# Hybrid trunk: raw input transposed at once, its norm applied to the products, and 32-tile products in the MLPs

## The chip, the core and the metric

The kernel runs on one core of one Trainium2 chip. The metric is the device time of one execution in microseconds (us), the median over runs. TensorE (PE) multiplies, VectorE (DVE), ScalarE (ACT) and GpSimd (POOL) work element by element, SyncE (SP) issues most DMAs; ACT and POOL issue some as well.

## The reference, cut to what matters

The input x is 256 tokens by 2048 channels, float32. Two layers follow each other, the first with a gated DeltaNet as token mixer, the second with sparse attention; behind each mixer stands an MLP.

```python
def rms_norm(x, g):
    y = xf * lax.rsqrt(jnp.mean(xf * xf, axis=-1, keepdims=True) + EPS)
    return (y * g.astype(jnp.float32)).astype(x.dtype)
...
    for i in range(DEPTH):
        u = rms_norm(h, norm_mix[i])
        if i % N_MIXERS == 0:
            mix = gated_deltanet(u, ...)
        else:
            mix = dsa_attention(u, ...)
        h = h + mix
        h = h + squared_relu_mlp(rms_norm(h, norm_mlp[i]), mlp_w_up[i], mlp_w_down[i])
    return rms_norm(h, norm_final)
```

In gated_deltanet the normed input is multiplied by w_in (12352 columns: q, k and v for a convolution and the delta rule, z for a gate, b and a for beta and decay). The factor rsqrt(mean) is one number per token, so it can be applied to x or to the products of x.

## The kernel before, in words

**Products.** Each weight and each activation is split into a rounded part and a rest ("hi" and "lo": whi, wlo, xhi, xlo), and a product is three matmuls (mm3, L321). by_channel (L359) holds weights stationary and streams 256 tokens: columns of 256, tiles named acc<-xhi,whi and the like. by_token (L377) holds activations stationary and streams weight columns: 512 wide (acc<-whi,h), or 256 wide for z.

**Weights.** Stream (L131) lists every weight block in order of use, 512 KB each. get() (L144) hands out the next one; on the way it issues the DMA of blocks further on (SP, tile raw), casts raw to whi on ACT and subtracts on DVE for wlo, three blocks ahead of use (four buffers each).

**Start.** Scope "first" (L402) loads x in four pieces of 128 x 1024 through SP, the identity, eight rows of gains, and then weights. It sums squares of all four pieces, computes rsqrt, scales x (normalise, L444), and a background generator first (L451) transposes 16 blocks k on PE, splitting each into xhi and xlo with the gain as factor. by_channel of group 0 uses the blocks as they come.

**DeltaNet.** 16 groups g of two heads (L736): by_channel gives q, k, v (192 matmuls), which ACT copies to s; by_token gives z (96 matmuls); group 0 has also the b and a columns (48 matmuls, read by decays, L480). The delta rule itself runs as background generators: delta (L520) per group, solved (L598) per pair of groups. solved inverts a triangular matrix with 32x32 and 64x64 products (aux<-Tc,yv, aux<-Lc,Tct and others), forms the output (the tile Tt), computes a factor f by rsqrt on POOL, multiplies Tt by f and the gate zg on DVE, transposes it on PE (aux<-wide,Tt) and splits it to the tile h.

**What sets the order.** Pace (L28) keeps a modelled clock per engine while the program is written. Background.tick (L122), called after each weight row of a product, emits the next step of a background chain when the model says that its inputs are there. ensure (L345) emits steps regardless, when a product needs their result now. Every engine then runs its instructions in the order in which they were written.

**After the groups.** early_chunks (L396) starts the output projection (512 wide, 6 matmuls per block k) on the 28 first blocks while the last pair is still solved; block 24 is the first that needs pair 6. Then come the MLP (mlp, L829: two halves, each of eight by_channel passes of 192 matmuls and four by_token chunks), the attention layer with its own products, and the second MLP. In the first pass of the first half, transposes of the last chunk (transposed, L787) are still mixed with the matmuls.

Of the kernel before, what the change touches and what calls it, by code (L numbers as in the profile page):

```python
# [14 lines left out]
P = 128  # L15
T = 256
# [114 lines left out]
class Stream:  # L131
# [8 lines left out]
    def add(self, shape, pieces, turn=None):  # L140

        self.items.append((shape, pieces, turn))

    def get(self):  # L144
        pace, i = self.pace, self.used
        self.used += 1
        ahead = min(self.ahead, i + 1)
        while self.split < min(i + ahead + 1, len(self.items)) or self.loaded < min(i + self.loads + 1, len(self.items)):
            while self.loaded < min(self.split + self.loads - self.ahead, len(self.items)):
                (n, w), pieces, _ = self.items[self.loaded]  # L150
                raw = self.raw_pool.tile([P, 1024], F32, name="raw")
                view = raw[:, : n * w].rearrange("p (n w) -> p n w", n=n)
                for at, src in pieces:
                    self.sync.dma_start(out=at(view), in_=src)
                self.raw[self.loaded] = raw
                self.loaded += 1
# [20 lines left out]
def tile_hybrid_trunk(ctx: ExitStack, tc: tile.TileContext, a: dict, out: bass.AP):  # L177
# [115 lines left out]
    def small_tile(n, name, dt=F32):  # L293
        return small.tile([P, n], dt, name=name)
# [104 lines left out]
        return [by_token(2, h_part(tiles), key, outs=o, k0=nk - 4) for o in outs]  # L399


    with tc.tile_pool(name="first", bufs=1) as fp:  # L402
        xin = fp.tile([P, 2, D], F32, name="xin")
        rows = fp.tile([P, P], F32, name="rows")
        cwr = fp.tile([P, 2, P], F32, name="cwr")
        quarters = [(tb, slice(c * 1024, c * 1024 + 1024)) for c in range(2) for tb in range(2)]
        for tb, s in quarters:
            sync.dma_start(out=xin[:, tb, s], in_=a["x"][0, tb * P:tb * P + P, s])
        sync.dma_start(out=ident, in_=a["consts"][:, 0:P])
        dve.memset(rows, 0.0)  # L410
        at = 0
        VEC = {}
        for name, src in (
            ("mix0", a["norm_mix"][0]), ("mlp0", a["norm_mlp"][0]), ("mix1", a["norm_mix"][1]), ("mlp1", a["norm_mlp"][1]),
            ("q", a["dsa_q_norm"][0]), ("kv", a["dsa_kv_norm"][0]), ("kidx", a["dsa_kidx_norm"][0]), ("out", a["dn_out_norm"][0]),
        ):
            n = src.shape[0] // P
            sync.dma_start(out=rows[at:at + n, :], in_=src.rearrange("(n p) -> n p", p=P))
            VEC[name] = at
            at += n  # L420
        pool.dma_start(out=cwr, in_=a["dn_conv_w"][0].rearrange("t (c p) -> (t c) p", p=P).rearrange("(n q) p -> q n p", q=P))
        pool.dma_start(out=upper, in_=a["consts"][:, P:2 * P])
        pool.dma_start(out=fine, in_=a["consts"][:, 2 * P:].rearrange("p (n c) -> p n c", c=B))

        def vec(name, i=0):
            return vecs[:, VEC[name] + i:VEC[name] + i + 1]

        sq4 = small_tile(4, "sq4")
        for n, (tb, s) in enumerate(quarters):
            junk = fp.tile([P, 1024], F32, name="junk", bufs=2)  # L430
            if n % 2 == 0:
                act.activation(junk, xin[:, tb, s], AF.Square, accum_out=sq4[:, n:n + 1])
            else:
                dve.scalar_tensor_tensor(junk, xin[:, tb, s], 1.0, xin[:, tb, s], op0=OP.mult, op1=OP.mult, accum_out=sq4[:, n:n + 1])
        rs = small_tile(2, "rs")
        sq = small_tile(2, "sq")
        dve.tensor_tensor(sq, sq4[:, 0:2], sq4[:, 2:4], op=OP.add)
        dve.tensor_scalar(sq, sq, 1.0 / D, EPS, op0=OP.mult, op1=OP.add)
        rsqrt(rs, sq, 2)
        tp = aux()  # L440
        pe.transpose(tp[:, 0:P], rows, ident)
        act.copy(vecs, tp[:, 0:72])

        def normalise(c):  # L444
            s = slice(c * 512, c * 512 + 512)
            act.activation(xin[:, 0, s], xin[:, 0, s], AF.Copy, scale=rs[:, 0:1])
            dve.tensor_scalar(xin[:, 1, s], xin[:, 1, s], rs[:, 1:2], None, op0=OP.mult)

        normalise(0)

        def first():  # L451
            for k in range(KD):
                t = aux()
                for tb in range(2):
                    pe.transpose(t[:, tb * P:tb * P + P], xin[:, tb, k * P:k * P + P], ident)
                split(t[:, :T], xT[0][:, k], xT[1][:, k], vec("mix0", k))
                ready.add(("x0", k))
                if k % 4 == 1 and k < 12:
                    normalise(k // 4 + 1)
                yield  # L460
            t = aux()
            for i in range(2):
                pe.transpose(t[:, i * P:i * P + P], cwr[:, i, :], ident)
            act.copy(cw, t[:, 0:T])

        bg.add(first())
        bg.step()
        bg.step()
        first_banks = by_channel(8, x_part, "x0", ahead=3)
        bg.drain()  # L470


    tokc = const.tile([P, 2, P], F32, name="tokc")
    GLM, BETA, GL = 32, 64, 96
    hT = []
    with tc.tile_pool(name="delta", bufs=2, reuse_waits="tile") as dp:
        gl_dram = dramp.tile([DN_H, T], F32, name="gl_dram")
        pairs = {}

        def decays(ps):  # L480
            q = slice(96, 128)
# [5 lines left out]
            act.activation(ba[64:96], ps[64:96, :T], AF.Tanh, scale=0.5)  # L487
# [3 lines left out]
            dve.tensor_scalar(xa, ps[q, :T], par[q, 1:2], None, op0=OP.add)  # L491
# [106 lines left out]
        def solved(p, la, r, rs, zg):  # L598
# [159 lines left out]
        chunks = early_chunks(hT, "o", 32, [[pkp.tile([P, 512], F32, name=f"pk{b}") for b in range(2)]])  # L758
        bg.drain()


    res = ctx.enter_context(tc.tile_pool(name="res", bufs=1, reuse_waits="tile"))
    x_scope = x_pool()
# [34 lines left out]
    def finish(outs, part, k0, scale, final):  # L798
# [6 lines left out]
        for tb in range(2):  # L805
# [20 lines left out]
            dve.scalar_tensor_tensor(x, x, rs, final[:, s], op0=OP.mult, op1=OP.mult)  # L826
            (act if tb else sync).dma_start(out=o, in_=x)

    def mlp(key, gain, next_key, final=None):  # L829
# [276 lines left out]
```

## Time and profile before

| | us |
|---|---|
| median of 3 runs (lowest, highest) | 2602.39 (2600.97, 2603.22) |
| the profiled execution | 2600.29 |
| its span in the trace | 2598.4 |
| PE busy | 2555.5 (98%) |
| DVE busy | 1535.6 (59%) |
| ACT busy | 1273.0 (49%) |
| POOL busy | 300.5 (12%) |

A matmul's end in the trace is modelled and overlaps the next one, so the distance from start to start is read as its cost. Stretches of the span: start and group 0 up to some 60 us, DeltaNet groups to 720 us, output projection to 933 us, first MLP to 1457 us and its last chunks to 1660 us, attention layer to 1884 us, second MLP to the end.

### The profile page before, as it was taken

The page shows a single profiled execution, that of the slowest core. Times are in us where ns is not written, and L with a number is a line of the kernel's source. Part 1 is how long each engine was busy: PE and PEld are TensorE (multiplying, and loading weights), DVE is VectorE, ACT ScalarE, POOL GpSimd, SP SyncE. Part 2 cuts the span into 40 slices and gives each one's busy share as a digit, 9 for nine tenths or more (in the row PEclk, how much of TensorE's full clock was granted, in tenths as well). Part 3 has the DMA queues.
Part 4 walks back from the last instruction along what each step waited for, and adds up shares of the span by engine and source line. Part 5 has one row for each costly group of instructions (what it writes and reads, how often), then busy time and mean ns, then how long its engine had stood idle before and what let it go on. Part 6 is the DMA issues. An engine that isn't in the chain of part 4 may idle for free.

```text
span 2598.4 us, 52409 instructions
## 1 busy us (share of the span) xinstructions
PE 2555.5 (98%) x21795; PEld 2342.0 (90%) x21795; DVE 1535.6 (59%) x2179; ACT 1273.0 (49%) x1890; POOL 300.5 (12%) x512
## 2 busy tenths in 40 slices
PE   7999999999999999999999999999999999999998
PEld 7999999999978799988899988898899988999886
DVE  5867677768764555554455555576555544455544
ACT  5555555555554544443344444566454433444443
POOL 0433344434331000000000000000000000000000
PEclk9999999999999999999999999999999999999999
DMA  6755555555554566666666666644666666666664
GB/s 193 195 148 152 143 146 157 146 154 151 153 167 145 173 192 193 194 192 194 194 186 180 194 187 191 183 131 146 177 189 194 194 194 193 189 187 185 193 194 150
DMA packets 325965, 455.91 MB, mean 175 GB/s; under 512 B 18344, under 2 KB 159904, under 8 KB 325344
## 3 DMA queue, kind: packets, MB, share of 16 engines
q1 hardware_dynamic: 322320, 444.11, 57.5%
q10 hardware_dynamic: 3072, 7.11, 0.9%
q8 instruction: 170, 2.79, 0.4%
q0 software_dynamic: 336, 1.34, 0.1%
q14 instruction: 67, 0.55, 0.1%
HBM read 450.37 MB, written 2.13 MB: 174 GB/s over the span
## 4 chain that ended last, share of the span: by engine, by line
PE 90%; DVE 5%; ACT 2%; issue 2%; DMA 1%; POOL 1%; SPq 0%; ACTq 0%; DVEq 0%; POOLq 0%
PE acc L81 81%; PE aux L81 5%; PE pk L81 3%; DVE wlo L81 2%; DVE Tct L81 1%; DVE y L81 1%; ACT Lc L81 1%; ACT whi L81 1%; DMA raw<-in_dn_w_in 0%; POOL rs_u L81 0%; DMA xin<-in_x 0%; POOL E L81 0%; DVE p L81 0%; DVE h L81 0%; DVE Tt L81 0%
## 5 line engine op out<-in xcount | busy, mean ns | idle before, releaser
L81 DVE TENSOR_TENSOR wlo<-raw,whi 128x1024 fp32r<-128x1024 f32 x838 | 1026.8, 1233 | 868.3 <-ACT whi L81 863.2
L81 ACT CAST whi<-raw 128x1024 fp32r<-128x1024 f32 x838 | 874.4, 1049 | 864.8 <-PE acc L81 815.8
L81 PE MATMUL acc<-xhi,whi 128*128 128x256 f32 x3088 | 870.5, 282 | 0.3 <-ACT whi L81 0.3
L81 PE MATMUL acc<-xhi,wlo 128*128 128x256 f32 x3088 | 860.1, 279 | 1.3 <-DVE wlo L81 1.3
L81 PE MATMUL acc<-xlo,whi 128*128 128x256 f32 x3088 | 860.2, 279 | 0.0
L81 PE MATMUL acc<-whi,h 128*128 128x512 f32 x2688 | 846.4, 392 | 4.0 <-ACT acc L81 2.0
L81 PEld LDWEIGHTS acc<-whi,h 128*128 128x128 f32 x2688 | 504.5, 188 | 111.3 <-ACT acc L81 2.9
L81 PEld LDWEIGHTS acc<-xhi,wlo 128*128 128x128 f32 x3088 | 584.7, 189 | 1.8 <-DVE wlo L81 1.8
L81 PEld LDWEIGHTS acc<-xhi,whi 128*128 128x128 f32 x3088 | 580.8, 188 | 2.8 <-ACT whi L81 0.7
L81 PEld LDWEIGHTS acc<-xlo,whi 128*128 128x128 f32 x3088 | 581.7, 188 | 0.2
L81 PE MATMUL acc<-wlo,h 128*128 128x512 f32 x1344 | 524.3, 390 | 0.0
L81 PEld LDWEIGHTS acc<-wlo,h 128*128 128x128 f32 x1344 | 252.6, 188 | 50.0
L81 PE MATMUL acc<-whi,xhi 128*128 128x256 f32 (+2 forms) x576 | 171.3, 297 | 0.0
L81 PE MATMUL acc<-whi,xlo 128*128 128x256 f32 (+2 forms) x576 | 166.1, 288 | 0.0
L81 PE MATMUL acc<-wlo,xhi 128*128 128x256 f32 (+2 forms) x576 | 165.9, 288 | 0.0
L81 POOL TENSOR_SCALAR E<-R,tokc 128x128 f32<-128x128 f32 x96 | 104.1, 1098 | 143.5 <-ACT y L81 79.2
L81 POOL DMA_DIRECT2D gain<-in_norm_final x1 | 0.6, 649 | 956.6 <-DVE nm L81 956.6
L81 PEld LDWEIGHTS acc<-whi,xhi 128*128 128x128 f32 x576 | 108.1, 188 | 2.6
L81 PEld LDWEIGHTS acc<-whi,xlo 128*128 128x128 f32 x576 | 108.2, 188 | 1.2
L81 PEld LDWEIGHTS acc<-wlo,xhi 128*128 128x128 f32 x576 | 108.1, 188 | 1.3
L81 DVE SCALAR_TENSOR_TENSOR y<-s,cw,y 128x255 f32<-128x255 f32 (+2 forms) x192 | 93.9, 489 | 13.1 <-ACT y L81 8.4
L81 POOL TENSOR_TENSOR h<-h,gain 128x512 f32<-128x512 f32 x6 | 7.6, 1290 | 736.5 <-ACT acc L81 736.5
(253 smaller groups left out, 1940.4 us busy)
## 6 DMA issues: line engine op xcount, KB each, us to landing
raw<-in_mlp_w_up SPq DMA_DIRECT2D x256, 512.0 KB, 4.4
raw<-in_mlp_w_down SPq DMA_DIRECT2D x256, 512.0 KB, 4.2
raw<-in_dn_w_in SPq DMA_DIRECT2D x66, 512.0 KB, 4.4
raw<-in_dn_w_in SPq DMA_DIRECT2D x256, 128.0 KB, 2.7
raw<-in_dn_w_in SPq DMA_DIRECT2D x128, 256.0 KB, 3.3
raw<-in_dn_w_out SPq DMA_DIRECT2D x64, 512.0 KB, 3.7
raw<-in_dsa_w_out SPq DMA_DIRECT2D x32, 512.0 KB, 3.9
raw<-in_dsa_w_uq SPq DMA_DIRECT2D x16, 512.0 KB, 3.7
```

Source lines behind the costliest of these rows:

```text
L81: r = f(*args, **kwargs)
```

## The change

Four edits.

1. x is loaded in four blocks of 512 channels for all tokens, the first through SP, three through ACT, whose queue also takes the first gains and the identity; the other gains go through POOL. Weight loads are issued on SP right behind the first block (fetch).
2. x is transposed raw. The squares and rsqrt run in the background behind the 16 transposes. The factor of a token is applied later: as a row (rs_row, made by a product of ones and a diagonal matrix) when q, k and v are taken from the banks (now on DVE) and in decays, as a scale of the tanh of z (rs_half), and as one more POOL multiplication of f in solved (rs0).
3. b, a and z of group 0 are computed inside the first scope, ahead of the taking of q, k and v. 20 products of ones are put on PE: 12 at the very start, 8 behind the first two transposed blocks.
4. In each MLP half one "visit" is put into the background: four 32x32 products whose result is read by nobody.

```diff
+    def fetch(self):
+        while self.loaded < min(self.split + self.loads - self.ahead, len(self.items)):
...
+                self.sync.dma_start(out=at(view), in_=src)
...
+        warm_up(12)
+        act.dma_start(out=rows[0], in_=a["norm_mix"][0].rearrange("(n p) -> n p", p=P))
+        act.dma_start(out=ident, in_=a["consts"][:, 0:P])
+        for c in range(4):
+            (act if c else sync).dma_start(out=xin[:, :, c * 512:c * 512 + 512],
+                                           in_=a["x"][0].rearrange("(b p) d -> p b d", p=P)[:, :, c * 512:c * 512 + 512])
...
+        ws.fetch()
...
-            if n % 2 == 0:
-                act.activation(junk, xin[:, tb, s], AF.Square, accum_out=sq4[:, n:n + 1])
-            else:
-                dve.scalar_tensor_tensor(junk, xin[:, tb, s], 1.0, xin[:, tb, s], op0=OP.mult, op1=OP.mult, accum_out=sq4[:, n:n + 1])
...
-        def normalise(c):
...
-            act.activation(xin[:, 0, s], xin[:, 0, s], AF.Copy, scale=rs[:, 0:1])
-            dve.tensor_scalar(xin[:, 1, s], xin[:, 1, s], rs[:, 1:2], None, op0=OP.mult)
...
+            for c in range(4):
+                squares(c)
+                yield
...
+            rsqrt(rs0, sq, 2)
+            dg = fp.tile([P, 2, P], F32, name="dg")
+            for tb in range(2):
+                dve.tensor_scalar(dg[:, tb], ident, rs0[:, tb:tb + 1], None, op0=OP.mult)
+            yield
+            t = aux()
+            pe.matmul(t[:, :T], lhsT=ones, rhs=dg.rearrange("p b c -> p (b c)"), start=True, stop=True)
+            act.copy(rs_row, t[:, :T])
...
         bg.step()
         bg.step()
+        warm_up(8)
         first_banks = by_channel(8, x_part, "x0", ahead=3)
+        first_ba = by_channel(2, x_part, "x0", n_ct=1)[0]
+        first_zo = by_token(4, x_part, "x0", n_cols=256)
         bg.drain()
...
+            pool.tensor_tensor(four(f), four(f), rs0.unsqueeze(1).unsqueeze(1).to_broadcast([P, 2, 2, 2]), op=OP.mult)
...
-                act.copy(s[:, 2 * c:2 * c + 2].rearrange("p n t -> p (n t)"), banks[c])
+                dve.tensor_tensor(s[:, 2 * c:2 * c + 2], banks[c].rearrange("p (n t) -> p n t", n=2),
+                                  rs_row.unsqueeze(1).to_broadcast([P, 2, T]), op=OP.mult)
             if g == 0:
-                bg.add(decays(by_channel(2, x_part, "x0", n_ct=1)[0]))
-            zo = by_token(4, x_part, "x0", n_cols=256)
+                bg.add(decays(first_ba))
+            zo = by_token(4, x_part, "x0", n_cols=256) if g else first_zo
...
-                act.activation(zg[:, b], zo[b], AF.Tanh, scale=0.5)
+                act.activation(zg[:, b], zo[b], AF.Tanh, scale=rs_half[:, b:b + 1])
...
+    def visit():
+
+        t = aux()
+        for q in range(4):
+            s = slice(B * q, B * q + B)
+            pe.matmul(t[s, 0:B], lhsT=ident[s, s], rhs=ident[s, s], start=True, stop=True)
+        yield
+
     def mlp(key, gain, next_key, final=None):
...
             for p in range(8):
+                if p == 1 - half:
+                    bg.add(visit())
                 banks = by_channel(8, x_part, key)
```

The start on ACT, before (junk is the sum of squares, xin<-xin the scaling by the norm, whi a weight's cast):

```order
L81 ACT_TABLE_LOAD
L81 ACTIVATE junk,sq_117<-xin 128x1024 x2
L81 COPY vecs<-aux 128x72
L81 ACTIVATE xin<-xin,rs 128x512
L81 ACTIVATE xhi<-aux,vecs 128x256 x2
L81 ACTIVATE xin<-xin,rs 128x512
L81 CAST whi<-raw 128x1024 x2
```

and in the change:

```order
L81 DMA rows_105<-in_norm_mix 16x128
L81 DMA wide<-in_consts 128x128
L81 DMA xin<-in_x 128x2x512 x3
L81 ACT_TABLE_LOAD
L81 COPY vecs<-aux 128x16
L81 ACTIVATE xhi<-aux,vecs 128x256 x2
L81 CAST whi<-raw 128x1024 x2
```

Squares and scaling are gone from ahead of the first weight cast; three loads of x are issued here.

The end of pair 6 on DVE, before (sc to f make the factor of the output, Tt<-Tt,f,zg applies it, h is the split that the projection reads, wlo a weight's rest):

```order
L81 TENSOR_TENSOR wlo<-raw,whi 128x1024 x4
L81 TENSOR_SCALAR sc<-rs_9310 128x2
L81 TENSOR_SCALAR sc<-rs_10162 128x2
L81 SCALAR_TENSOR_TENSOR s_11255<-sc 128x4
L81 TENSOR_TENSOR so<-so,s_11255 128x8
L81 TENSOR_SCALAR so<-so 128x8
L81 TENSOR_SCALAR rs_t<-so 128x8
L81 TENSOR_SCALAR f<-rs_t 128x8
L81 TENSOR_TENSOR wlo<-raw,whi 128x1024 x3
L81 SCALAR_TENSOR_TENSOR Tt<-Tt,f,zg 128x128 x8
L81 TENSOR_TENSOR wlo<-raw,whi 128x1024
L81 SCALAR_TENSOR_TENSOR h<-aux,vecs,h 128x512
```

and in the change:

```order
L81 TENSOR_TENSOR wlo<-raw,whi 128x1024 x4
L81 TENSOR_SCALAR sc<-rs_9550 128x2
L81 TENSOR_SCALAR sc<-rs_10311 128x2
L81 SCALAR_TENSOR_TENSOR s_11362<-sc 128x4
L81 TENSOR_TENSOR so<-so,s_11362 128x8
L81 TENSOR_SCALAR so<-so 128x8
L81 TENSOR_SCALAR rs_t<-so 128x8
L81 TENSOR_SCALAR f<-rs_t 128x8
L81 SCALAR_TENSOR_TENSOR Tt<-Tt,f,zg 128x128 x8
L81 SCALAR_TENSOR_TENSOR h<-aux,vecs,h 128x512
```

The four weight rests that stood among these steps are no longer there. PE in the change, at the same place, from the last output products of pair 6 (aux<-yv,la) to its transposes:

```order
L81 MATMUL aux<-yv,la_10374 128x128 x2
L81 MATMUL aux<-yv,la_10375 128x128
L81 MATMUL acc<-whi,h 128x512
L81 MATMUL acc<-wlo,h 128x512
L81 MATMUL acc<-whi,h 128x512 x2
L81 MATMUL acc<-wlo,h 128x512
L81 MATMUL acc<-whi,h 128x512
L81 MATMUL aux<-wide,Tt 128x128 x4
```

Six matmuls of the projection stand between the two; before, 54 did. The transposes stand ahead of block 24 of the projection in both.

## Rows read from the trace of the kernel before

**Rows 1.** Stretches, acc alone: us, PE busy (count), PEld, DVE, ACT, PEclk (granted clock), DMA, GB/s
```profile
20.04:22.62 2.58, 2.50 (x10) 2.28 (x11) 0.00 (x0) 0.00 (x0) 1.00 0.64 165
1000.00:1050.00 50.00, 50.00 (x444) 50.00 (x443) 3.48 (x6) 2.98 (x5) 1.00 0.59 181
1350.00:1400.00 50.00, 50.00 (x427) 50.00 (x426) 4.13 (x6) 3.21 (x6) 1.00 0.59 181
2350.00:2400.00 50.00, 50.00 (x427) 50.00 (x426) 2.75 (x4) 2.38 (x4) 1.00 0.59 178
```

**Rows 2.** Timeline of PE around 32-tile products: start, us, instruction, count
```profile
137.65 0.28 PE L81 MATMUL acc<-xhi,wlo 128*128 128x256 f32 x1
...
139.06 0.28 PE L81 MATMUL acc<-xhi,wlo 128*128 128x256 f32 x1
139.27 0.75 PE L81 MATMUL aux<-Tc,yv 32*32 32x32 f32 x64
...
140.17 0.28 PE L81 MATMUL acc<-xlo,whi 128*128 128x256 f32 x1
...
141.32 0.28 PE L81 MATMUL acc<-xhi,wlo 128*128 128x256 f32 x1
...
696.89 0.75 PE L81 MATMUL aux<-Lc,Tct 32*32 32x32 f32 x64
```

**Rows 3.** Timelines of DVE, ACT and PE at the start
```profile
6.61 1.22 DVE L81 SCALAR_TENSOR_TENSOR junk<-xin 128x1024 f32<-128x1024 f32 x1 [5.48 <-DMA xin<-in_x]
...
10.87 1.22 DVE L81 SCALAR_TENSOR_TENSOR junk<-xin 128x1024 f32<-128x1024 f32 x1 [3.03 <-DMA xin<-in_x]
...
18.76 2.36 DVE L81 TENSOR_TENSOR wlo<-raw,whi 128x1024 fp32r<-128x1024 f32 x2 [0.64 <-ACT whi L81]
...
17.69 1.99 ACT L81 CAST whi<-raw 128x1024 fp32r<-128x1024 f32 x2
...
20.04 0.58 PE L81 MATMUL acc<-xhi,wlo 128*128 128x256 f32 x1 [0.46 <-DVE wlo L81]
...
22.62 0.56 PE L81 MATMUL acc<-xhi,whi 128*128 128x256 f32 x1
...
24.31 0.38 PE L81 MATMUL aux<-wide,xin 128*128 128x128 f32 x2
...
25.92 0.38 PE L81 MATMUL aux<-wide,xin 128*128 128x128 f32 x2
```

**Rows 4.** DeltaNet, 100 to 720 us: two groups of instructions, PE's waits; timeline at 77 us
```profile
L81 ACT COPY s<-acc 128x512 f32<-128x512 f32 x28 | 15.5, 583 | 7.2 <-PE acc L81 6.5
...
L81 DVE SCALAR_TENSOR_TENSOR la<-E,wj,pk 128x512 f32<-128x512 f32 x29 | 20.2, 737 | 0.0
...
PE aux L81 <- DVE Tc L81: 5.9, 9, 1.6
...
77.04 0.44 PE L81 MATMUL aux<-wide,E 128*128 128x128 f32 x2 [1.49 <-DVE E L81]
```

**Rows 5.** Timelines of PE, ACT, POOL and DVE at the end of pair 6
```profile
747.18 1.50 PE L81 MATMUL aux<-yv,la 128*128 128x128 f32 x12
748.44 0.48 PE L81 MATMUL acc<-whi,h 128*128 128x512 f32 x1
...
761.16 1.03 PE L81 MATMUL aux<-wide,Tt 128*128 128x128 f32 x4 [0.22 <-DVE Tt L81]
...
764.71 0.73 PE L81 MATMUL acc<-whi,h 128*128 128x512 f32 x2 [1.01 <-DVE h L81]
...
748.72 0.59 ACT L81 COPY Tt<-aux 128x512 f32<-128x512 f32 x1 [1.24 <-PE aux L81]
...
754.06 1.13 POOL L81 TENSOR_TENSOR rs_u<-f 128x8 f32<-128x8 f32 x1 [13.84 <-DVE f L81]
...
759.41 1.22 POOL L81 TENSOR_TENSOR f<-f,sc 128x8 f32<-128x8 f32 x1
...
760.66 2.19 DVE L81 SCALAR_TENSOR_TENSOR Tt<-Tt,f,zg 128x128 f32<-128x128 f32 x8
```

More of the change, by code (lines that the diff above doesn't have):

```diff
@@ L142, in add @@
         self.items.append((shape, pieces, turn))
+    def fetch(self):
+        while self.loaded < min(self.split + self.loads - self.ahead, len(self.items)):
+            (n, w), pieces, _ = self.items[self.loaded]
+            raw = self.raw_pool.tile([P, 1024], F32, name="raw")
+            view = raw[:, : n * w].rearrange("p (n w) -> p n w", n=n)
+            for at, src in pieces:
+                self.sync.dma_start(out=at(view), in_=src)
+            self.raw[self.loaded] = raw
+            self.loaded += 1
     def get(self):
@@ L148, in get @@
         while self.split < min(i + ahead + 1, len(self.items)) or self.loaded < min(i + self.loads + 1, len(self.items)):
[L149 to L156, printed above, removed]
+            self.fetch()
             if self.split >= min(i + ahead + 1, len(self.items)):
@@ L399, in early_chunks, with warm_up, vec @@
         return [by_token(2, h_part(tiles), key, outs=o, k0=nk - 4) for o in outs]
+    carry = ExitStack()
+    carried = carry.enter_context(tc.tile_pool(name="carried", bufs=1))
+    tokc = carried.tile([P, 2, P], F32, name="tokc")
+    rs0 = carried.tile([P, 2], F32, name="rs0")
+    rs_half = carried.tile([P, 2], F32, name="rs_half")
+    rs_row = carried.tile([P, T], F32, name="rs_row")
     with tc.tile_pool(name="first", bufs=1) as fp:
         xin = fp.tile([P, 2, D], F32, name="xin")
-        rows = fp.tile([P, P], F32, name="rows")
+        rows = [fp.tile([n, P], F32, name=f"rows{n}") for n in (16, 56)]
         cwr = fp.tile([P, 2, P], F32, name="cwr")
[L406 to L410, printed above, removed]
+        def warm_up(n):
+            warm = aux()
+            for _ in range(n):
+                pe.matmul(warm[:, 0:P], lhsT=ones, rhs=ones, start=True, stop=True)
+        warm_up(12)
[4 more added lines that the diff above has]
+                                           in_=a["x"][0].rearrange("(b p) d -> p b d", p=P)[:, :, c * 512:c * 512 + 512])
+        pool.dma_start(out=cwr, in_=a["dn_conv_w"][0].rearrange("t (c p) -> (t c) p", p=P).rearrange("(n q) p -> q n p", q=P))
+        pool.dma_start(out=upper, in_=a["consts"][:, P:2 * P])
+        pool.dma_start(out=fine, in_=a["consts"][:, 2 * P:].rearrange("p (n c) -> p n c", c=B))
+        def vec(name, i=0):
+            return vecs[:, VEC[name] + i:VEC[name] + i + 1]
+        sq8 = small_tile(8, "sq8")
+        ws.fetch()
         at = 0
@@ L417, in tile_hybrid_trunk, with vectors, squares @@
             n = src.shape[0] // P
-            sync.dma_start(out=rows[at:at + n, :], in_=src.rearrange("(n p) -> n p", p=P))
+            if at:
+                pool.dma_start(out=rows[1][at - 16:at - 16 + n, :], in_=src.rearrange("(n p) -> n p", p=P))
             VEC[name] = at
             at += n
[L421 to L430, printed above, removed]
-            if n % 2 == 0:
-                act.activation(junk, xin[:, tb, s], AF.Square, accum_out=sq4[:, n:n + 1])
-            else:
-                dve.scalar_tensor_tensor(junk, xin[:, tb, s], 1.0, xin[:, tb, s], op0=OP.mult, op1=OP.mult, accum_out=sq4[:, n:n + 1])
[L435 to L442, printed above, removed]
-        def normalise(c):
+        def vectors(i, s):
+            tp = aux()
+            n = s.stop - s.start
+            pe.transpose(tp[:, 0:n], rows[i], ident[0:n, 0:n])
+            act.copy(vecs[:, s], tp[:, 0:n])
+        vectors(0, slice(0, 16))
+        def squares(c):
             s = slice(c * 512, c * 512 + 512)
-            act.activation(xin[:, 0, s], xin[:, 0, s], AF.Copy, scale=rs[:, 0:1])
-            dve.tensor_scalar(xin[:, 1, s], xin[:, 1, s], rs[:, 1:2], None, op0=OP.mult)
-        normalise(0)
+            junk = fp.tile([P, 2, 512], F32, name="junk", bufs=2)
+            act.activation(junk[:, 0], xin[:, 0, s], AF.Square, accum_out=sq8[:, c:c + 1])
+            dve.scalar_tensor_tensor(junk[:, 1], xin[:, 1, s], 1.0, xin[:, 1, s], op0=OP.mult, op1=OP.mult,
+                                     accum_out=sq8[:, 4 + c:5 + c])
         def first():
@@ L457, in first @@
                 ready.add(("x0", k))
-                if k % 4 == 1 and k < 12:
-                    normalise(k // 4 + 1)
                 yield
+            for c in range(4):
+                squares(c)
+                yield
+            sq = small_tile(2, "sq")
+            dve.tensor_reduce(sq, sq8.rearrange("p (b c) -> p b c", b=2), axis=AX.X, op=OP.add)
+            dve.tensor_scalar(sq, sq, 1.0 / D, EPS, op0=OP.mult, op1=OP.add)
+            rsqrt(rs0, sq, 2)
[7 more added lines that the diff above has]
+            yield
             t = aux()
@@ L464, in first @@
             act.copy(cw, t[:, 0:T])
+            vectors(1, slice(16, 72))
         bg.add(first())
@@ L468, in tile_hybrid_trunk @@
         bg.step()
+        warm_up(8)
         first_banks = by_channel(8, x_part, "x0", ahead=3)
+        first_ba = by_channel(2, x_part, "x0", n_ct=1)[0]
+        first_zo = by_token(4, x_part, "x0", n_cols=256)
         bg.drain()
-    tokc = const.tile([P, 2, P], F32, name="tokc")
     GLM, BETA, GL = 32, 64, 96
@@ L478, in tile_hybrid_trunk @@
         pairs = {}
+        dve.tensor_scalar(rs_half, rs0, 0.5, None, op0=OP.mult)
         def decays(ps):
@@ L486, in decays @@
             dve.memset(ba, 0.0)
-            act.activation(ba[64:96], ps[64:96, :T], AF.Tanh, scale=0.5)
+            dve.tensor_tensor(ba[64:96], ps[64:96, :T], rs_row[64:96], op=OP.mult)
+            act.activation(ba[64:96], ba[64:96], AF.Tanh, scale=0.5)
             dve.tensor_scalar(ba[64:96], ba[64:96], 0.5, 0.5, op0=OP.mult, op1=OP.add)
@@ L490, in decays @@
             xa, e, z, p = (w[q, i] for i in range(4))
-            dve.tensor_scalar(xa, ps[q, :T], par[q, 1:2], None, op0=OP.add)
+            dve.tensor_tensor(xa, ps[q, :T], rs_row[q], op=OP.mult)
+            dve.tensor_scalar(xa, xa, par[q, 1:2], None, op0=OP.add)
             dve.scalar_tensor_tensor(e, xa, -1.0, xa, op0=OP.mult, op1=OP.max)
@@ L759, in tile_hybrid_trunk @@
         bg.drain()
+    carry.close()
     res = ctx.enter_context(tc.tile_pool(name="res", bufs=1, reuse_waits="tile"))
@@ L827, in finish @@
             (act if tb else sync).dma_start(out=o, in_=x)
+    def visit():
[3 more added lines that the diff above has]
+            pe.matmul(t[s, 0:B], lhsT=ident[s, s], rhs=ident[s, s], start=True, stop=True)
+        yield
     def mlp(key, gain, next_key, final=None):
```

## The prediction, made before the change was run

> **What bounds the kernel now.** I read the table of busy times first: PE is busy for 98% of the span, the next engine (DVE) for 59%. So a change moves the time only through the number of matmuls, the distance between them, or the few places where PE stands still. Then the stretches of acc matmuls, for the distance. In the first half of an MLP 444 matmuls start in 50 us, 112.6 ns each; in the second half 427, 117.1 ns each, in the first MLP and in the second alike [rows 1]. The granted clock is 1.00 in all of them, so the 4.5 ns are not the clock. The reader should see that PE is full in both and still has two paces. Then PE's timeline around 32x32 products in DeltaNet: 12 matmuls take 1.41 us ahead of them (137.65 to 139.06, 117.5 ns each), and the ten distances behind (140.17 to 141.32) are 115 ns with the first, slower ones among them [rows 2]. I went through 28 such places from 139.27 to 696.89 us, these two being the first and the last. Where the same kind of matmul goes on, the short distance follows in 26. Most (22) had it already, but of the five that came at the long distance four left at the short one. Last, the timelines of the start, of DeltaNet's waits and of the end of pair 6 [rows 3, 4, 5].
>
> **The start.** Before, PE flows from 20.04, released by the first weight rest: whi 1.0 us (two in 1.99), then wlo 1.2 us (two in 2.36) [rows 3]. The weights were issued behind x, the norm and the gains. Of x, the second piece of 512 KB was in use at 6.61 and the fourth at 10.87 [rows 3], so 1 MB takes 4.3 us. In the change the weights follow the first megabyte of x on SP while ACT's queue brings the other three blocks beside them. If the queues share evenly, the first weights are there when 2.1 MB have landed, at about 10.9, and 2.2 us of whi and wlo make 13.2: **-6.8**. Ends: weights as soon as the first block, flow at 9.4 (-10.6); weights behind all of x, 15.3 (-4.7). The transposes need one x block, no norm, and are ahead of that. The squares, now beside the matmuls, cost DVE and ACT the same two to four us that they had free.
>
> Between 20.04 and 22.62 ten matmuls and two transposes start in 2.58 us; from 24.31 to 25.92 twelve and two take 1.61 [rows 3]. At the later pace the first set would take 14/12 less, 1.38 us: the slow beginning costs 1.2. The granted clock in that stretch is 1.00 too [rows 1], so only the distances (0.21 us beside 0.11) show it; they look like the lower of the two levels, 1.2 and 2.4 GHz. The change puts 20 products of ones ahead, yet there is still waiting between the last of them and the first wlo. I take half: **-0.6** (0 to -1.2).
>
> **DeltaNet.** The taking of s moves from ACT, 583 ns each, to DVE, where the nearest row of that shape is 737 ns; it is 32 times on either [rows 4], some 24 us on an engine that is 60% busy. PE waited 5.9 us for DVE (nine waits for Tc between 100 and 720 us) [rows 4]. A DVE that has a quarter more to do ahead of these steps makes them later by perhaps a fifth, +1.3; the first taking of a bank in group 1 by 0.15 us for each of four banks, +0.7; the wait of 1.49 for E at 77.04 [rows 4] may vanish, since z, b and a of group 0 now stand ahead, -1.5. Together **+0.5**, ends -3 (the nine waits halve as well) and +6 (they double).
>
> **The end of pair 6.** The last output products of pair 6 begin at 747.18 and the transposes of Tt stand at 761.16, where PE waits only 0.22 us [rows 5]. In between goes a chain: ACT's copy at 748.72, POOL's factor from 754.06 to its last multiplication at 759.41 (1.22 us), DVE's Tt at 760.66. PE covers it with 54 projection matmuls from 748.44 on, 12.50 us without the wait, 0.231 us each. The written order of the change leaves six of them there: the chain is emitted later against PE, the model steps it on time only until block 24 forces it, and block 24 comes first. So 48 matmuls (11.1 us) of cover are gone, and POOL has one more multiplication in the chain (12 steps take 5.35 us from 754.06 to 759.41, so +0.45). What PE no longer does there it does later, hence this is time: +11.55. The wait for h at 764.71, 1.01 us [rows 5], goes, because the weight rest ahead of h is no longer there: **+10.5**. Ends: +8.5, if DVE without its four weight rests is 2 us earlier with Tt; +11.6.
>
> After such a stall PE may come back at the pace of the start, whose price was 1.2 [rows 3]: **+1.2**, ends 0 and +1.4. The Trainium skill, "TensorE: Matmul & The Clock Gate", Part 1, says that the half rate is the default and that an idle PE is put back to it; by that rule the term stands, without it the sum is 1.2 less.
>
> **The visits.** In half 1 the visit stands behind the first 12 matmuls of 1536 and 1524 follow: 2 x 1524 x 4.5 ns = -13.7 [rows 1]. In half 0 the pace is short already, and the visit leaves it so. One visit costs what the 64 products at 139.27 cost beyond their number: from 139.06 to 140.17 pass 1.11 us, less one distance 0.99; 0.75 of it are the 64 (12 ns each, four take 0.05), 0.24 the change over and back [rows 2]. So 0.3 each, 1.2 for four (0.2 to 4.0): **-12.5**. Their aux tile is free and nobody waits for it.
>
> **Sum** against the profiled execution, 2600.3: -6.8 - 0.6 + 0.5 + 10.5 + 1.2 - 12.5 = -7.7, so 2592.6. The median of the runs is 2.1 above that execution: **2594.7 us**. The other edits (rs_half, rs_row in decays) replace an operand, at the same count of instructions, and cost nothing.
>
> **Rivals.**
> (a) Visits only cost. For: in 22 of 26 places the short pace was there before, so the products may have caused nothing. Against: four of five long ones became short. The -13.7 goes: 2608.4. The Trainium skill, "TensorEngine Tiling (Array Packing)", Key Properties, speaks for it: a change of the tiling mode drains PE, and it promises nothing for what follows. The 0.24 us agree with a drain; whether that is all, the trace before cannot say.
> (b) Slower: a visit leaves the long pace wherever it stands. Place: pass 1 of half 0, behind which 1332 matmuls run at the short one in each MLP; it decides if the pace falls with the first matmuls behind the visit. 2 x 1332 x 4.5 ns = 12.0, plus the lost 13.7: 2620.4. For: transposes flip the pace in either direction, and at one place in DeltaNet the long one stayed. Against: 22 of 23 short ones stayed short.
> (c) Mixed: half 1 is mended, half 0 spoiled: 2606.7.
> (d) The stall at pair 6 does not come, or the chain is short: without its 11.7 it is 2583.0. For: the chain may be hidden by something that the written order doesn't show. Against: PE runs in that order, and six matmuls are 1.4 us.
>
> **How the numbers follow.** The forecast with its own range, 2587 to 2602 from the ends above, gets 0.60; (a) 0.15, (b) 0.08, (c) 0.07, (d) 0.10. 0.2% of 2602.4 is 5.2 us, about what a measurement of this kernel can tell from no change: faster is below 2597.2, slower above 2607.6. Faster: (d) 0.10 and most of the forecast, 0.43. Same: the rest of it, 0.17, half of (a) and most of (c), 0.10. Slower: (b), half of (a) and a bit of (c), 0.20. The range 2584 to 2609 leaves out (b) and half of (d), and a little more at either end.
>
> **What the profile after would show.** The first row of steady matmuls near 13.2 us. 444 matmuls per 50 us in both halves of both MLPs; if 427 in half 1, (a) holds; if 427 in half 0, (b) or (c). One wait of PE of 10 to 12 us for Tt near the end of pair 6, and 0.2 us distances behind it. s on DVE near 0.7 us, PE's waits for Tc between 4 and 10 us. Wrong would be the prediction if DVE became what PE waits for in most groups, if the weights landed behind all of x, or if the pace in DeltaNet's own stretches moved, which I did not cost.

## The result, and the profile after

The changed kernel takes 2644.91 us (median of four runs, 2643.84 to 2646.61) against 2602.19 for the one before: 1.0164 times as long, 95% interval 1.0152 to 1.0176. Forecast was 2594.7, a little faster. The page of its profiled execution, span and busy times:

```profile
span 2642.4 us, 52603 instructions
...
PE 2593.6 (98%) x21870; PEld 2369.8 (90%) x21870; DVE 1558.6 (59%) x2215; ACT 1255.9 (48%) x1860; POOL 289.1 (11%) x527
```

PE is as full as before and 38 us longer busy, with 75 matmuls more. Waits are not in the busy time, so the matmuls themselves are slower. The acc stretches of the first MLP after the change, first a stretch of half 0, then one of half 1, with the columns of [rows 1]:

```profile
1000.00:1050.00 50.00, 50.00 (x427) 50.00 (x426) 2.75 (x4) 2.38 (x4) 1.00 0.61 183
1350.00:1400.00 50.00, 50.00 (x427) 50.00 (x426) 2.75 (x4) 2.38 (x4) 1.00 0.62 192
```

Half 0 had 444 in 50 us before [rows 1] and has 427 now; half 1 has 427 still, in spite of its visit. PE's timeline around the visit of half 0 (the four products are recorded as eight):

```profile
983.97 0.28 PE L81 MATMUL acc<-xlo,whi 128*128 128x256 f32 x1
984.09 0.28 PE L81 MATMUL acc<-xhi,wlo 128*128 128x256 f32 x1
984.30 0.26 PE L81 MATMUL pk<-wide 32*32 32x32 f32 x8
984.49 0.39 PE L81 MATMUL acc<-xhi,whi 128*128 128x256 f32 x1
984.71 0.28 PE L81 MATMUL acc<-xlo,whi 128*128 128x256 f32 x1
984.83 0.28 PE L81 MATMUL acc<-xhi,wlo 128*128 128x256 f32 x1
```

The distance is 0.12 us on either side. So half 0 was slow before its visit came; the visit did not make it so, and did not mend it. From 984.09 to 984.49 pass 0.40 us, less one distance 0.28, and the next matmul is 0.1 us late: the visit costs some 0.4 us, where 0.3 was forecast.

The start, timelines of ACT and PE:

```profile
10.84 1.05 ACT L81 CAST whi<-raw 128x1024 fp32r<-128x1024 f32 x1 [1.76 <-DMA raw<-in_dn_w_in]
14.19 1.05 ACT L81 CAST whi<-raw 128x1024 fp32r<-128x1024 f32 x1 [2.31 <-DMA raw<-in_dn_w_in]
...
13.20 0.39 PE L81 MATMUL acc<-xhi,wlo 128*128 128x256 f32 x1 [0.75 <-DVE wlo L81]
...
16.95 0.44 PE L81 MATMUL aux<-wide,xin 128*128 128x128 f32 x2 [2.31 <-DVE xlo L81]
...
18.25 0.41 PE L81 MATMUL acc<-xhi,whi 128*128 128x256 f32 x1
18.46 0.42 PE L81 MATMUL acc<-xlo,whi 128*128 128x256 f32 x1
```

The first weights are there at 10.84 (forecast 10.9) and the flow begins at 13.20 (forecast 13.2; 20.04 before, [rows 3]). But the second weights come only at 14.19; ACT, which waits for them, cannot make the next xhi, PE stands still for 2.31 us, and behind that the distance is 0.21 us. The stretches of that place and of the one behind the stall of pair 6 (us, PE busy, PEld, DVE, ACT, POOL, then the granted clock, DMA share and GB/s):

```profile
17.60:20.60 3.00, 3.00 (x17) 3.00 (x16) 2.22 (x3) 2.58 (x4) 0.00 (x0) 0.50 0.81 228
...
787.87:790.00 2.13, 2.13 (x5) 1.66 (x6) 0.73 (x1) 0.00 (x0) 0.00 (x0) 0.50 0.00 0
```

Here the granted clock is 0.50, the lower of the two levels, each time behind a wait of PE. The first of the two is no fixed part of the change: in a_pad896 (below), which has the same instructions in the same order, PE waits 2.06 us at this place and the clock stays at 1.00 behind it:

```profile
17.60:20.60 3.00, 3.00 (x29) 3.00 (x28) 2.35 (x3) 2.52 (x5) 0.00 (x0) 1.00 0.74 213
```

The end of pair 6 on PE:

```profile
774.65 1.50 PE L81 MATMUL aux<-yv,la 128*128 128x128 f32 x12
775.90 0.48 PE L81 MATMUL acc<-whi,h 128*128 128x512 f32 x1
...
777.14 0.40 PE L81 MATMUL acc<-whi,h 128*128 128x512 f32 x1
785.92 1.17 PE L81 MATMUL aux<-wide,Tt 128*128 128x128 f32 x4 [8.38 <-DVE Tt L81]
787.87 0.80 PE L81 MATMUL acc<-whi,h 128*128 128x512 f32 x1 [0.78 <-ACT h L81]
788.46 0.63 PE L81 MATMUL acc<-wlo,h 128*128 128x512 f32 x1
```

Six matmuls stand in the gap, as the written order had it, and PE waits 8.38 us where it waited 0.22 [rows 5]; behind it the matmuls are 0.4 to 0.6 us apart instead of 0.23. The chain behind it is shorter than before, 10.0 us from 775.90 to 785.92 where it was 12.7. POOL's part, first and last step:

```profile
781.52 0.20 POOL L81 TENSOR_TENSOR rs_u<-f 128x8 f32<-128x8 f32 x1 [13.59 <-DVE f L81]
...
785.19 0.20 POOL L81 TENSOR_TENSOR f<-f,rs 128x8 f32<-128x8 f32 x1
```

All 14 steps take 0.20 us. Before, the first and the last took 1.13 and 1.22 [rows 5], and each of the three long ones ran while DVE worked on a weight rest; here no rest stands in the gap. The rests before, and the third long step:

```profile
753.90 1.23 DVE L81 TENSOR_TENSOR wlo<-raw,whi 128x1024 fp32r<-128x1024 f32 x1
756.62 1.23 DVE L81 TENSOR_TENSOR wlo<-raw,whi 128x1024 fp32r<-128x1024 f32 x1 [1.49 <-ACT whi L81]
759.34 1.22 DVE L81 TENSOR_TENSOR wlo<-raw,whi 128x1024 fp32r<-128x1024 f32 x1 [1.49 <-ACT whi L81]
...
756.70 1.21 POOL L81 TENSOR_SCALAR rs_u<-rs_u 128x8 f32<-128x8 f32 x1
```

This holds for the whole trace of the kernel before: the 80 POOL operations of this form that begin while DVE stands free take 0.20 us, the 23 that begin during a weight rest take 1.05 to 1.27 and end 0.06 us behind the rest.

PE's waits between 100 and 720 us (in total, times, longest):

```profile
PE aux L81 <- DVE Tc L81: 9.7, 6, 1.9
PE aux L81 <- DVE Tt L81: 2.6, 6, 0.4
PE acc L81 <- DVE wlo L81: 1.4, 5, 0.5
```

Tc was 5.9 [rows 4].

What the prediction had not looked at is where the tiles stand in memory. The change takes tokc (1024 bytes per partition) out of the pool "const" at the bottom and leaves 128 bytes more in "small"; so raw, whi, wlo and h all stand 896 bytes lower. xhi and xlo hang from the top and stay. The addresses of the built programs, in bytes per partition:

```
            before   change   remainder by 256: before, change
whi         40480    39584    32   160
wlo         56864    55968    32   160
one h      101920   101024    32   160
xhi        172000   172000   224   224
xlo        188384   188384   224   224
```

So whi stood 64 bytes above xhi by the remainder of 256 before the change, and 192 above it (64 below) after; wlo and xlo stand like them.

### The profile page after: what moved, and what is told of

Same layout as the page of the kernel before. It is cut to its first block, busy times and chain, and to the rows that moved or that the text cites. A ratio compares the mean times of both kernels' runs of the same rounds, so it can differ in the third digit from the quotient of the medians.

```text
span 2642.4 us, 52603 instructions
## 1 busy us (share of the span) xinstructions
PE 2593.6 (98%) x21870; PEld 2369.8 (90%) x21870; DVE 1558.6 (59%) x2215; ACT 1255.9 (48%) x1860; POOL 289.1 (11%) x527
## 4 chain that ended last, share of the span: by engine, by line
PE 84%; issue 5%; DVE 5%; POOL 2%; ACT 2%; DMA 1%; SPq 0%; ACTq 0%; DVEq 0%; POOLq 0%
PE acc L81 77%; PE aux L81 4%; PE pk L81 3%; DVE wlo L81 2%; POOL rs_u L81 1%; DVE y L81 1%; DMA raw<-in_dn_w_in 1%; DVE Tct L81 1%; ACT whi L81 1%; POOL E L81 1%; POOL f L81 1%; DVE s L81 0%; DMA xin<-in_x 0%; ACT s L81 0%; ACT Lc L81 0%
## 5 line engine op out<-in xcount | busy, mean ns | idle before, releaser
L81 POOL TENSOR_SCALAR E<-R,tokc 128x128 f32<-128x128 f32 x96 | 96.4, 1017 | 89.3 <-ACT y L81 84.0
```

What stands on the lines that cost most here:

```text
L81: r = f(*args, **kwargs)
```

## The experiments

### Move the tiles alone

```diff
     ones = const.tile([P, P], F32, name="ones")
+    const.tile([P, 224], F32, name="pad")
```

**a_pad896**: the changed kernel with this line. 

> The changed kernel with one unused tile of 896 bytes per partition ahead of the small pool, so that the weight buffers, the tiles h and all pools behind them stand at the addresses of the kernel before (they had moved down by 896 bytes, while xhi and xlo stayed where they were). The instructions and their order do not change. Theory A (the pace of the 256-column matmuls hangs on where the weights stand against xhi and xlo): half 0 of both MLPs runs at 113 ns again, 2 x 6.5 us less, DeltaNet gets back 3 to 5 us of its own pace, the 512-wide stretches 1 to 3 us: 2622 to 2632 us. If the visits work in this layout, half 1 runs at 113 too, and it is 2609 to 2618. Theory B (the visits, or the other order of the work, made half 0 slow): half 0 stays at 117.8, and the time within 3 us of the changed kernel's 2644.9.

**b_low896**: the kernel before, moved the other way.

```diff
+    const.tile([P, 32], F32, name="pad")
...
+    carry = ExitStack()
+    carried = carry.enter_context(tc.tile_pool(name="carried", bufs=1))
+    tokc = carried.tile([P, 2, P], F32, name="tokc")
...
-    tokc = const.tile([P, 2, P], F32, name="tokc")
```

> The kernel before with its weight buffers and the pools behind them moved down by 896 bytes (tokc is taken from a pool of its own behind them, 128 bytes of padding stand ahead), as the change moved them; instructions and order as before. Theory A: half 0 of both MLPs falls to 117.8 ns, 2 x 6.5 us, DeltaNet's own pace loses 3 to 5, the 512-wide stretches 1 to 3: 2619 to 2625 us. Theory B: nothing changes, 2600 to 2604.

Measured: a_pad896 2608.79 us, ratio to before 1.0024 (1.0014 to 1.0033): 36 us of the change are gone with 896 unused bytes. b_low896 2624.03 us, 1.0079 (1.0064 to 1.0094): 21 us more than the kernel before, whose half 1 had no short pace to lose. Their stretches, a_pad896 first:

```profile
1000.00:1050.00 50.00, 50.00 (x444) 50.00 (x443) 3.44 (x5) 2.98 (x5) 1.00 0.58 182
1350.00:1400.00 50.00, 50.00 (x444) 50.00 (x443) 3.04 (x5) 2.38 (x4) 1.00 0.58 184
```

and b_low896:

```profile
1000.00:1050.00 50.00, 50.00 (x427) 50.00 (x426) 2.75 (x4) 2.38 (x4) 1.00 0.63 192
1350.00:1400.00 50.00, 50.00 (x427) 50.00 (x426) 2.75 (x4) 2.38 (x4) 1.00 0.62 193
```

The shift gives and takes half 0's pace in either kernel, with no instruction moved: of the two theories A holds, B is out. In a_pad896 half 1 is at 444 too: at these addresses its visit works. Comparing when the same matmul starts in the changed kernel and in a_pad896, the 35.2 us between their spans come from DeltaNet and what is ahead of it (5.7), half 0 of the two MLPs (7.2 and 7.3), half 1 (7.0 and 6.9), and 1.1 from the rest.

### The visits alone

```diff
             for p in range(8):
+                if p == 1 - half:
+                    bg.add(visit())
```

**a_novisit** leaves these out of the changed kernel, **b_visits** adds them (and visit itself) to the kernel before, nothing else.

> The changed kernel without the four visits. Theory A: the visits do nothing but cost their 0.3 us each, half 0 stays at 117.8 ns without them: 2643 to 2645 us. Theory B: without the visits half 0 is back at 113 ns in its last seven passes: 2631 to 2633.

> The kernel before with the four visits and nothing else. Theory A says nothing on half 1, where the layout allows both paces: if a visit sets the short one, 13.7 less 1.2 is gained, 2589 to 2591 us; if not, it costs 1.2: 2602 to 2605, and half 0 stays at 113. Theory B: half 0 falls to 117.8 behind the visit: 2613 to 2617.

a_novisit: 2642.44 us (2640.35 to 2642.88), ratio 1.0148 (1.0133 to 1.0164), just under theory A's 2643 and 9 us above theory B's 2633. b_visits: 2590.55 us, ratio 0.9951 (0.9936 to 0.9965). The stretches of b_visits:

```profile
1000.00:1050.00 50.00, 50.00 (x444) 50.00 (x443) 4.13 (x6) 3.58 (x6) 1.00 0.61 190
1350.00:1400.00 50.00, 50.00 (x444) 50.00 (x443) 4.13 (x6) 3.57 (x6) 1.00 0.59 187
```

The visits are worth 12.2 us at the addresses of the kernel before, where 12.5 was forecast, and at those of the change they only cost: 2.5 us by the medians, which the two intervals do not tell from the 1.2 forecast. By its median b_visits is the fastest version of all that compute the reference: both kernels are beaten by adding 32-tile products to the old one.

### Which distance is good

My next idea was that the short pace comes when both operands have the same remainder, since the 512-wide matmuls are at 227 ns where theirs agree. Paddings of other sizes (the same line), at first on the kernel before and on the change:

**b_low64.** 

> The kernel before with its weight buffers and all pools behind them 64 bytes lower, made like the run with 896 bytes (other padding), instructions and order as before. Where the addresses stand: xhi, xlo and the last two tiles h at 32 bytes below a multiple of 512, whi, wlo and the other tiles h at 32 above one in the kernel before, at 160 above one in the change, and here at 32 below one, as xhi. In the kernel before the 512-wide matmuls run at 227 ns where both operands have the same remainder, and at 229 to 232 with the last two tiles h. Theory A1 (the short pace comes whenever both operands of a matmul have the same remainder by 512): all halves of both MLPs at 113 ns without any visit, 13.6 less, DeltaNet 5 to 9 less, the 512-wide stretches 1 to 2: 2577 to 2584 us. Theory A2 (a shift only draws the pace of each stretch anew): at least one half, or DeltaNet's own stretches, slower than that: 2590 to 2625.

**a_pad832.** 

> The changed kernel with 832 bytes of padding, which is 64 less than the run with 896: whi, wlo and h have the remainder of xhi. Theory A1: all at the short pace, so 2608.8 less 1 to 5 in DeltaNet and 1 to 2 in the 512-wide stretches: 2601 to 2607 us. Theory A2: anything from 2608 to 2645.

**a_pad576.** 

> The changed kernel with 576 bytes of padding: whi, wlo and h have the remainder of xhi by 256, but not by 512. If 256 is the period, it reads like the run with 832 bytes, 2601 to 2607 us; if not, half 0 and half 1 of the MLPs are at 117.8 ns, about 2645, or mixed between.

It was wrong, and clearly: b_low64 2641.73 us (1.0151, 1.0136 to 1.0166), a_pad832 2657.93 (1.0212, 1.0197 to 1.0227), a_pad576 2659.5 (one execution). The stretch of half 0 in b_low64:

```profile
1000.00:1050.00 50.00, 50.00 (x419) 50.00 (x419) 2.75 (x4) 2.37 (x4) 1.00 0.61 187
```

419 in 50 us, a third pace of 119.3 ns by this count and 120.0 from start to start, in both halves; in a_pad832 DeltaNet's by_channel runs at 120.0 as well. Equal remainders are among the worst places for these matmuls, and in a_pad832 the visits do nothing. a_pad832 and a_pad576 are 256 bytes apart and alike.

The other distances were tried on a_cover (its order is told below; its padding is 896):

**c_pad704.** 

> The run with the new order of the projection, but 704 bytes of padding in place of 896: whi, wlo and h stand 128 bytes away from xhi by remainder of 256. Seen so far: 0 apart, all 256-column matmuls of by_channel at 120.0 ns; 64 above xhi, either 113.3 or 117.8, and a visit sets 113.3; 192 above xhi (64 below), 117.8 nearly always. Theory P1 (the farther apart, the better): 113.3 everywhere, DeltaNet gets its 5.4 us of slower pace back: 2588 to 2592 us. Theory P2 (64 above is a lucky place): slower than 2596.2, up to 2635 where all are at 120.0 or 117.8.

**c_pad864.** 

> The same with 864 bytes: 32 above xhi by remainder of 256. Theory P1: between 0 and 64 apart, so mostly 117.8 to 120.0: 2615 to 2635 us. Theory P2: no order, anything between 2590 and 2635.

**c_pad640.** 

> The new order of the projection with 640 bytes of padding: 64 above xhi by remainder of 256, as with 896, but 256 bytes lower. If the remainder by 256 (or less) decides: MLP halves at 113.3 ns, 2594 to 2599 us. If the whole distance, or a longer period, decides: halves at 117 to 120, 2615 to 2645.

**c_pad672.** 

> The same with 672 bytes: 96 above xhi by remainder of 256. Known: 64 above gives 113.3 with a visit, 128 above 118.7. If a band around 64 is good, 113.3 and 2594 to 2600; if 64 alone, 117 to 119 and 2625 to 2640.

**c_pad736.** 

> The same with 736 bytes: 160 above xhi by remainder of 256, between 128 (118.7 ns) and 192 (117.8). Expected between them, 2628 to 2640 us; if the pairs 64 apart from each other share something, no reason for 113.3 here.

| whi above xhi by remainder of 256 | runs | matmuls in 50 us from 1000 and from 1350 | time of the runs on a_cover, us |
|---|---|---|---|
| 0 | b_low64, a_pad832, a_pad576 | 419, 419 (b_low64) | |
| 32 | c_pad864 | 425, 425 | 2634.06 |
| 64 | before, b_visits, a_pad896, a_cover, c_pad640 | 444, 427 without a visit; 444, 443 or 444 with | 2596.19 and 2596.12 |
| 96 | c_pad672 | 428, 424 | 2636.39 |
| 128 | c_pad704 | 424, 424 | 2638.88 |
| 160 | c_pad736 | 419, 419 | 2650.11 |
| 192 | the change, a_novisit, b_low896 | 427, 427 | |

c_pad864, c_pad640, c_pad672 and c_pad736 are one execution each. c_pad640 stands 256 bytes lower than a_cover and takes the same time, well within the scatter of a_cover's runs (2594.09 to 2597.56): the remainder by 256 decides, not the distance as such. P1 (the farther the better) falls with c_pad704, which is slower than P2's 2635 too, and the band that c_pad672 looked for is not there: of the seven distances tried, 64 alone lets a visit set 113 ns. c_pad736 was expected between its neighbours, at 2628 to 2640, and is slower than both.

In all these runs whi moved and xhi stayed, so whi's own place would explain the table as well. The matmuls of z speak against it. There the activations are stationary and the weights stream, so the distance of the stationary from the moving operand is 192 where by_channel has 64, and 64 where it has 192. I counted, between 100 and 730 us, behind how many groups of 32-tile products (48 or 64 of them) the short pace follows (a median under 116 ns) where the same kind of matmul goes on:

| run | by_channel, distance | short behind | z, distance | short behind |
|---|---|---|---|---|
| before | 64 | 25 of 26 | 192 | 4 of 16 |
| b_low896 | 192 | 3 of 26 | 64 | 16 of 16 |
| a_pad896 | 64 | 31 of 33 | 192 | 3 of 16 |
| the change | 192 | 7 of 33 | 64 | 12 of 16 |

The two kinds change places with the shift. If whi's own place counted, it would have to be good in one role and bad in the other; the stationary operand's distance from the moving one fits both. No run moved xhi. At 160 and 96 it fits as well: at 160 by_channel has 120 ns (MLPs of c_pad736) and z 120 (c_pad672), at 96 by_channel 117 to 119 (c_pad672) and z 118 (c_pad736). For 224, which no run has for by_channel, z in c_pad864 gives 117 ns. Why 64 is good, and why the pace lasts over hundreds of matmuls once it is set, these runs don't tell.

### The end of pair 6

**a_cover**: a_pad896 with the projection in another order.

```diff
+        head = ([(0, 0, 24), (1, 0, 24), (0, 24, 28), (1, 24, 28), (2, 0, 28)] if nk == 32 else [(c, 0, late) for c in early])
...
+        if nk == 32:
+            outs = [by_token(12, h_part(tiles), key) for _ in range(2)]
+            for o in outs:
+                by_token(2, h_part(tiles), key, outs=o, k0=24)
+            outs.append(by_token(14, h_part(tiles), key, outs=banks[0]))
```

> The changed kernel with 896 bytes of padding and another order of the output projection: the first 24 blocks of chunks 0 and 1, then blocks 24 to 27 of both, then chunk 2, so that 144 matmuls more stand ahead of the first use of pair 6. The step of the prediction on pair 6 (a chain that has lost its cover): the wait of 8.4 us for Tt goes to under 1, and the doubled distances behind it too: 2608.8 less 9 to 12, 2597 to 2600 us. The rival (the wait comes from DVE's or POOL's new work, and moves with it): it comes back at another place, 2606 to 2611.

2596.19 us, ratio 0.9971 (0.9961 to 0.9981), 12.6 less than a_pad896. PE's waits between 717 and 960 us, where Tt led the list with 8.4:

```profile
PE aux L81 <- DVE Tc L81: 2.0, 2, 1.5
PE acc L81 <- ACT acc L81: 1.0, 1, 1.0
```

Tt is not among them any more, and it did not come back elsewhere; 12.6 is a little over the 9 to 12 expected. The lost cover is shown as the cause.

### DVE's new load in DeltaNet

**c_sact**: a_cover with the takings of s back on ACT.

```diff
-                dve.tensor_tensor(s[:, 2 * c:2 * c + 2], banks[c].rearrange("p (n t) -> p n t", n=2),
-                                  rs_row.unsqueeze(1).to_broadcast([P, 2, T]), op=OP.mult)
+                act._engine.copy(s[:, 2 * c:2 * c + 2].rearrange("p n t -> p (n t)"), banks[c])
+                pace.note("dve", "tensor_tensor", (s[:, 2 * c:2 * c + 2],), {})
```

(The second line keeps the modelled clocks as they were, so that the order stays.) 

> The run with the new order of the projection, with the 32 takings of s back on ACT, as plain copies; what is left out is the token's factor on q, k and v. The order of PE's instructions and of POOL's is the same, only DVE loses 32 operations of 0.67 us and ACT gets 32 of 0.58. The prediction's step on DeltaNet (DVE's new load delays what PE waits for): PE's waits in DeltaNet go from 17 back to 11 us as before the change: 2596.2 less 5 to 8, 2588 to 2591. The rival (the waits come from the other order of steps, and from more interruptions): within 2 of 2596.2.

2586.38 us, 9.8 less than a_cover. Its waits from 100 to 720 us:

```profile
PE aux L81 <- DVE Tc L81: 7.3, 8, 1.1
PE aux L81 <- DVE Tt L81: 2.6, 6, 0.4
PE aux L81 <- ACT Lc L81: 1.6, 6, 0.7
```

In a_cover they were 9.5 for Tc and 2.7 for wlo. Matmul by matmul, DeltaNet takes 9.7 us less here than in a_cover. Of these 5.8 are waits of PE (17.35 to 11.53 in all of DeltaNet, added up from the trace). Another 1.4 stand from 163.33 to 166.74 us, where a_cover's granted clock reads 0.50 behind a wait of 1.78 us for Tc; here it reads 1.00 all through DeltaNet. The rest I can't assign. DVE's load is shown as the cause of that cost, at more than the 5 to 8 us expected.

**c_pool**: the same plain copies, and the factor applied behind them on POOL.

```diff
+                act.copy(s[:, 2 * c:2 * c + 2].rearrange("p n t -> p (n t)"), banks[c])
+                pool.tensor_tensor(s[:, 2 * c:2 * c + 2], s[:, 2 * c:2 * c + 2],
+                                   rs_row.unsqueeze(1).to_broadcast([P, 2, T]), op=OP.mult)
```

> The run with the new order of the projection (896 bytes of padding), with q, k and v taken from the banks by ACT as plain copies and multiplied by the token's factor on POOL, in place. It computes everything. DVE is as free as in the run with the plain copies (2586.4), POOL gets 32 operations, of 1.05 us or a little more each by its 128x256 rows, at the head of each group's chain. Theory: the chain has that much time to spare, 2586 to 2590 us. Rival: POOL or the longer chain becomes what PE waits for: 2596 or more.

2611.10 us, ratio 1.0028 (1.0018 to 1.0039): the rival. The new operation on POOL, and PE's wait, from 100 to 720 us:

```profile
L81 POOL TENSOR_TENSOR s<-s,rs_row 128x512 f32<-128x512 f32 x26 | 38.1, 1488 | 46.3 <-ACT s L81 46.3
...
PE aux L81 <- DVE Tc L81: 16.3, 7, 3.2
```

Each takes 1.49 us and lies in the chain, and PE's wait for Tc goes from 9.5 to 16.3. All waits of DeltaNet together are 24.2 us, 6.8 more than in a_cover. The larger part of the 14.9 us is the clock: from waits of 1.5 to 3.2 us on the granted clock of DeltaNet reads 0.50 for 27.3 us in all (3.4 in a_cover), PE is busy in 25.5 of them, and at half pace that is, by estimate, 13 us lost against 2. Two of these stretches, the first behind PE's wait of 3.22 us for Tc at 161.04:

```profile
162.18:165.59 3.41, 3.41 (x76) 3.12 (x75) 2.26 (x3) 2.74 (x4) 1.53 (x2) 0.50 0.54 127
...
551.30:554.71 3.41, 3.41 (x76) 3.12 (x75) 2.87 (x4) 3.41 (x5) 0.45 (x1) 0.50 0.70 191
```

The order was planned anew here, so its share isn't told apart.

## Why the prediction was wrong, and where it was right

**The pace of the MLPs** was the step that failed, in both halves of the term for the visits: "In half 0 the pace is short already, and the visit leaves it so", and half 1's -13.7. Both took the short pace as a state that transposes and 32-tile products set. It is that only at some addresses, and the prediction put their shift at nothing, without a look. The change moved whi by 896 bytes against xhi: half 0 fell to 117.8 ns, which costs 14.5 us in the two MLPs; half 1 stayed at 117.8 in spite of its visits, so 13.9 of the forecast gain did not come; and 5.7 were lost ahead of the MLPs, 3.7 in DeltaNet, whose pace suffers too, and 2.0 in the start, where the low clock stands in the one trace and not in the other. The 36 us are shown by moving nothing but the addresses, and b_low896 shows the loss in the other direction. That DeltaNet's own pace might move the prediction had named as a sign of being wrong. Of the rivals, (b) had the price of a spoilt half 0, but from a wrong mechanism: it laid it on the visit, and in the trace the pace is long ahead of it.

The trace of the kernel before held the sign. The prediction's 26 short ones in 28 places fit by_channel (25 of 26 in the count above); for z, with the operands in the other roles, the short pace follows the same products in 4 of 16 places. So the products alone do not set the pace.

**The visits** at the old addresses came out as reckoned: -12.5 forecast, -12.2 measured in the kernel before. Rival (a), that they only cost, holds at the addresses of the change. The rule of the Trainium skill that was put beside it ("TensorEngine Tiling (Array Packing)", Key Properties: a change of the mode drains PE) fits the 0.28 us ahead of the next matmul; a visit's gain, 113 against 118 ns behind it, lies outside that rule.

**DeltaNet** was the second miss, in size: +0.5 (ends -3 and +6) forecast. DVE's 32 new operations alone are worth 9.8 us. I scaled the waits that were there; the load also made new ones (wlo), and a longer wait can put the clock down behind it (the 1.4 us in a_cover). The rs_row in decays, called a replaced operand, is two DVE operations more, once.

**The start** fell short of its ends: -6.8 and -0.6 forecast, -4.7 at the least; where group 0 ends, a_pad896 is 4.5 us ahead of the kernel before and the changed kernel 2.6. The flow began at 13.20 as worked out, and at full pace, but a wait for the second weights gave part back (2.31 us, and 2.06 in a_pad896), and in the changed kernel's trace the 0.50 clock behind it too. The step took the first weight for the whole supply.

**Pair 6** was right in its mechanism: +10.5 and +1.2 forecast, 12.6 measured by giving the cover back. That the sum fits so well is partly luck, since both parts were off. The wait is 8.4, not 11.6: the chain is 2.7 us shorter, near the lower end of the step, but because POOL's steps are no longer slowed beside weight rests, and not because DVE is earlier. 12.6 less the 8.2 by which the wait grew leaves 4.4. In a_pad896 the granted clock is 0.50 for 10.2 us around this place and PE is busy in 6.2 of them, so some 3 us of it (an estimate) are the clock, where 1.2 was allowed; the rest is what else the new order saved. That the clock falls behind an idle PE, as "TensorE: Matmul & The Clock Gate" (Part 1) of the Trainium skill has it, is seen here behind the 8.4 us; behind the waits of some 2 us it is seen in one trace and not in another.

Without the 36 us of the addresses the change is 14 above the forecast: 2.9 from the start, 9.3 from DeltaNet, 0.9 from pair 6 and 0.3 from the visits, which leaves 0.7, less than the runs of a_pad896 scatter (2606.80 to 2613.89).

## What to carry to other kernels

Before costing a change by its instructions, list the addresses of the tiles that PE reads before and after it: a moved constant can slow thousands of matmuls (here those of 256 columns by 4%, while the 512-wide ones stay at 227 to 229 ns), and padding undoes it. Where one kind of matmul has two paces in a trace, treat the pace as something that the layout allows, and try some paddings of 32 bytes apart before anything else. A chain written by a modelled clock needs its cover counted again whenever work ahead of it moves. And where a change makes waits of PE longer, look at the granted clock behind them, not only at the waits.

## What the runs showed of the hardware

Four things that I had not expected. The distance of 256-column matmuls (weights whi or wlo, moving xhi or xlo) hangs on where the two stand by the remainder of 256 bytes: in the MLP halves 120.0 ns at 0 apart, 113.3 or 117.8 at 64, 117.8 at 192, and at no other distance tried 113.3 for a whole half. At 64 the pace is set by what PE did just before: behind a visit 113.3 ns for the 1524 matmuls that follow, without one 117.8 for all 1536 (half 1 of b_visits and of the kernel before). POOL's 128x8 operations took 0.20 us alone and 1.05 to 1.27 where a weight rest of 1.23 us ran on DVE at the same time. And the granted clock fell to 0.50 behind short waits of PE, though not behind all of them: in the changed kernel at 17.54 us (wait of 2.31) and at 543.19 (wait of 1.55, and matmuls of 256 columns 0.21 us apart behind it), in c_pool six times in DeltaNet (in or behind waits of 1.51 to 3.22); in a_pad896 not behind the 2.06 us at the start, and in the kernel before, with waits of up to 1.8 us, nowhere between 100 and 720 us. What decides it these rows don't show.
